# A causal mask as a minimum on VectorE, and another order of the small matmuls among the projection groups

## The chip, the cores and the metric

The kernel runs on one core of a Trainium2 chip. The metric is the time of one execution on the device, in microseconds (us). The engines are TensorE (PE in the rows; PEld is its weight load), VectorE (DVE), ScalarE (ACT), GpSimd (POOL) and SyncE (SP), which issues the DMAs here.

## What is computed

One decoder layer on 512 tokens of width 1024, float32. Cut to what matters:

```
h    = rms_norm(x, g_pre);  proj = h @ w_in        # 1664 RWKV columns, 1536 for q, k, v, 1024 gates
RWKV, 8 heads of 64, token by token:
   Sa = S a_t;  S = S * w_t + Sa b_t^T + v_t k_t^T;  y_t = S r_t
   then a norm per head, times lnx_w plus lnx_b, plus (r.k.r_k) v
attention, 8 heads of 64: logits = q k^T / 8 - slope * (t - s) for s <= t, else -1e30; softmax; times v
   (2 blocks of 256 with both always selected: plain causal attention)
y    = concat(y_rwkv, y_attn) * silu(gates)
out  = x + rms_norm(y @ w_out, g_post)
```

## The kernel before

Tokens lie along the free axis (512 columns) and features on the partitions, except for the attention's V and the output. A projection of 128 columns is made in full precision from two halves of each operand: weights and activations are split into a high part and a rest (`whi`, `wlo`, `xhi`, `xlo`), and three products are summed in PSUM (line 246). One product over 512 features, four matmuls of 128x512, is called a projection **group**; a projection of 128 columns is six groups. The split of a weight tile is a copy on ScalarE (line 230) and a subtraction on VectorE (line 231).

The RWKV half is done in chunks of 64 tokens. For each of four pairs of heads, `rwkv_keys` (line 359) makes decays and keys, with `ends` products for norms (396) and four transposes (405), and `rwkv_pairs` (423) makes the products within a chunk: transposes (437), products of 64x128 (444), the masked copy on VectorE (446), and two products for the bonus (462). `rwkv_inverse` (482) inverts 32x32 triangular blocks by a loop on VectorE, sends them through DRAM (502 to 511), and then **merges** the blocks by four quarters of 32x32 matmuls (514 to 534), each followed by copies on ScalarE and VectorE. `rwkv_chain` (542) takes eight steps, one per chunk: the state products (AR, 568), their copies, the u product (575) and its two copies (576, 577), the values of the next chunk (579), the update with BT (584), and the rest of the outputs (591).

The attention takes pairs of heads (`attn_pair`, 689): a stage for the row maxima (704 to 708), whose result is put into the operands, and then for each head and key block j the scores of 512-128j queries (732, 733), a mask product `tri` on the diagonal block (734), the exponential on ScalarE (736), and one step later the products with V (726). Afterwards four transposes and the gate (755).

The output projection (`half`, 820) runs in nine pieces of up to 512 columns, each with an RWKV half g=0 and an attention half g=1; `early_out` (833) issues the first half of pieces 0 and 1, the loop from line 892 the rest, with `AHEAD` pieces begun early.

TensorE's program order is written by a planner: the small parts are generators that yield (ns, wait), and `side` (107) resumes one when a virtual clock has reached its due time; `stream` (120) calls it after each projection group, at most two or three at a time. `PLAN` sets the order of the projections, and `PENDING` how many of them may be issued after q1 before the chain must be finished. The waits in the yields thus move instructions; TensorE then runs them in that order. The other engines' orders come from the framework's scheduler. PSUM slots are rings: two of p, three of s, two of c, one of r.

Of the kernel before, what the change touches and what calls it, by code (L numbers as in the profile page):

```python
# [9 lines left out]
F32 = mybir.dt.float32  # L10
# [27 lines left out]
PS = {"p": 2, "s": 3, "c": 2, "r": 1}  # L38
WARM = 9
PLAN = "k1 r1 k2 r2 k3 r3 v1 v2 v3 V q0 c0 G4 G5 q1 c1 q2 c2 G6 q3 c3 G7 G0 G1 G2 G3"  # L40
PENDING, AHEAD = 8, 5
MM = 232.0


# [1 line left out]
def hybrid_layer(ctx, tc, x, xt, params, ranks, w_in, w_v, w_out, g_post, out):  # L46
# [28 lines left out]
    def mps(tag="c"):  # L75
        return kept(pm, (512,), F32, tag, "ps_" + tag, PS[tag])
# [123 lines left out]

    dist = cst.tile([128, 10, 128], mybir.dt.bfloat16, name="dist")
    alibi = cst.tile([128, NH, NB], F32, name="alibi")
    tri = cst.tile([128, 2, 128], mybir.dt.bfloat16, name="tri")

    def attn_constants():
        for b in range(NB):
            o = b * (b + 1) // 2
            nc.gpsimd.iota(dist[:, o:o + b + 1, :], pattern=[[128, b + 1], [1, 128]], base=-256,
                           channel_multiplier=0, allow_small_or_imprecise_dtypes=True)
            nc.gpsimd.affine_select(out=dist[:, o + b, :], in_=dist[:, o + b, :], pattern=[[-1, 128]],  # L210
                                    compare_op=ALU.is_ge, fill=256.0 * NEG, base=0, channel_multiplier=1)
        nc.gpsimd.iota(alibi[:, 0, :], pattern=[[128, NB]], base=-256, channel_multiplier=1,
                       allow_small_or_imprecise_dtypes=True)
        for h in range(NH - 1, -1, -1):
            nc.vector.tensor_scalar(alibi[:, h, :], alibi[:, 0, :], 2.0 ** -(h + 1), None, ALU.mult)
        nc.vector.tensor_copy(tri[:, 0, :], ident)
        nc.gpsimd.memset(tri[:, 1, :], NEG)
        nc.gpsimd.affine_select(out=tri[:, 1, :], in_=tri[:, 1, :], pattern=[[-1, 128]], compare_op=ALU.is_gt,
                                fill=0.0, base=0, channel_multiplier=1)

    attn_constants()

# [136 lines left out]
    def rwkv_keys(p, ps):  # L359
# [2 lines left out]
        k = shifted(ps, 4 + p)  # L362
        sq = t2()
        nc.scalar.activation(sq, k, AF.Square, scale=col(KK + p))
        yield 0, 0 if p else 4000
        th = []
        for i in range(2):
            ps = mps()
# [19 lines left out]
        nc.scalar.activation(E[:, :, 1:C + 1], L.rearrange("p (c t) -> p c t", t=C), AF.Exp)  # L388
        en = at()
        nc.scalar.activation(en, L, AF.Exp, scale=-1.0)  # L390
        yield 4 * MM, 5500


        ps = mps()
# [28 lines left out]
    def rwkv_pairs(p, ps):  # L423
        g, q = p // 2, p % 2
        r = shifted(ps, p)
        yield 0, 0
        while keys[p] is None:
            yield 0, 300
        (k, E), BK = keys[p], BKs[:, q]
        ar, bt, am = AR[g][:, q], BT[g][:, q], Am[p]  # L430
        nc.vector.tensor_mul(ar[:, :, 1, :], v3(r), E[:, :, 1:C + 1])
        yield 0, max(4000, since[p] + 13000 - clock[0])
        msk = flat(mask).unsqueeze(1).to_broadcast([128, 4, 128])
        for c0 in (0, 4):
            ps = mps("r")
            for c in range(4):
                tr(ps[:, 128 * c:128 * c + 128], flat(BK[:, c0 + c]))
            acp(bt[:, c0:c0 + 4, :], ps.rearrange("p (c n) -> p c n", c=4))
            yield 900, 0
            pe = [mps("s") for _ in range(2)]  # L440
            for c in range(4):
                for e in range(2):
                    h = slice(64 * e, 64 * e + 64)
                    mm(pe[e][:, 128 * c:128 * c + 128], flat(BK[h, c0 + c]), flat(ar[h, c0 + c]), start=True, stop=True)
            for e in range(2):
                nc.vector.tensor_mul(am[:, e, c0:c0 + 4].rearrange("p c a b -> p c (a b)"),
                                     pe[e].rearrange("p (c n) -> p c n", c=4), msk)
            if c0:
                for hf in range(2):
                    d = slice(32 * hf, 32 * hf + 32)  # L450
                    nc.sync.dma_start(bd[hf, p].rearrange("n s t -> s n t"),
                                      am[d, :, :, 0, d].rearrange("s e c t -> s (e c) t"))
                paired[p] = True
            yield 1800, 2200
        nc.vector.scalar_tensor_tensor(r, r, col(RK + p), k, ALU.mult, ALU.mult)
        rk = [ring("kx", 2, T, dt=F32R) for _ in range(2)]
        acp(rk[0], r)
        nc.vector.tensor_sub(rk[1], r, rk[0].bitcast(F32))
        yield 0, 1500
        ps = mps("r")  # L460
        for i in range(2):
            mm(ps, bones_r, rk[i], start=(i == 0), stop=(i == 1))
        acp(bonus[p], ps)
        bon[p] = True
        yield 2 * MM, 0
# [16 lines left out]
    def rwkv_inverse():  # L482
# [31 lines left out]
        for g in range(2):  # L514
# [5 lines left out]
                           xq[0:32, 2 * g + q, e, c, :], start=True, stop=True)  # L520
            for e in range(2):
                (acp, vcp)[e](xq[32:64, 2 * g:2 * g + 2, e], px[64 * e + 32:64 * e + 64])
            yield 1700, 0
        for g in range(2):
            px = mps().rearrange("s (q c t) -> s q c t", q=2, t=32)
            for q in range(2):
# [4 lines left out]
            for q in range(2):  # L531
                for e in range(2):
                    (acp, vcp)[e](Am[2 * g + q][0:32, e, :, 0, 32:64], px[64 * e:64 * e + 32, q])
            yield 1700, 0
        ready["inverse"] = True
        yield 0, 800

# [4 lines left out]
    def rwkv_chain():  # L542
# [20 lines left out]
        for c in range(NCH):  # L563
# [5 lines left out]
                           stop=(s == 0 and p == NP - 1), skip_group_check=True)  # L569
            acp(uv[lo, 0], ry[0][lo])  # L570
            vcp(uv[lo, 1], ry[1][hi])
            yield 900 * (c > 0), 700
            u = mps()[:, 0:NP * HD].rearrange("p (q i) -> p q i", i=HD)
            for h, p, e in heads:
                mm(u[rows(e), p, :], Am[p][lo, e, c, 0, :], uv[lo, e, p, :], start=True, stop=True)
# [1 line left out]
            vcp(uv[lo, 1], u[hi])  # L577
            if not last:
                rn = values_in(c + 1)
            yield 500 + 1000 * (not last), 100  # L580
            if not last:
                d = mps()[:, 0:NP * HD].rearrange("p (q i) -> p q i", i=HD)
                for h, p, e in heads:
# [105 lines left out]
    def attn_pair(p):  # L689
# [29 lines left out]
        for e in range(2):  # L719
# [2 lines left out]
            PT = [None] * NB  # L722

            def times_values(j):
                for b in range(j, NB):
                    mm(po[:, b, 0:65], PT[j][:, 128 * (b - j):128 * (b - j) + 128], V[0][:, j, h, 0:65],
                       start=(j == 0 and b == 0), stop=(j == b), skip_group_check=True)

            for j in range(NB):
                n, cs = T - 128 * j, slice(128 * j, 128 * j + 128)  # L730
                ps = mps("s")
                mm(ps[:, 0:n], kx[e][:, cs], qx[e][:, 128 * j:T], start=True, stop=False)
                mm(ps[:, 0:n], kb[e][:, cs], qb[e][:, 128 * j:T], start=False, stop=False)
                mm(ps[:, 0:128], tri[:, 0, :], tri[:, 1, :], start=False, stop=True)
                PT[j] = t2()
                nc.scalar.activation(PT[j][:, 0:n], ps[:, 0:n], AF.Exp, scale=2.0 ** -(h + 1), bias=alibi[:, h, j:j + 1])  # L736
                yield 2 * MM * n / T + 80, 0
                if j:
                    times_values(j - 1)
                    yield 220 * (NB - j + 1), 0  # L740
# [67 lines left out]
    def out_weights():  # L808
        for k in range(8):
# [1 line left out]
                yield 0, 300  # L811
            wout(k)
            ready["wout"] = k
            yield 0, 1500

    xb = x[0].rearrange("(b p) d -> p b d", p=128)
    pieces = [(b, c) for b in range(NB) for c in ((0, 512), (512, 1024))][:-1] + [(NB - 1, (512, 768)), (NB - 1, (768, 1024))]
# [15 lines left out]
    def early_out():  # L833
# [4 lines left out]
            ys[0] = [t[:, i, :] for i in range(4)]  # L838
        for p in range(NP):
            gated(p, bonus[p])  # L840
        yield 0, 8000
        for i in range(2):
            for n in half(i, 0):
                yield 4 * MM, 0
# [51 lines left out]
    for b in range(NB):  # L896
# [2 lines left out]
        xs = [load_w(xb[:, b, 512 * n:512 * n + 512]) for n in range(2)]  # L899
        os = [at() for _ in range(2)]  # L900
        for j, i in enumerate(mine):
            if i + AHEAD < len(pieces):
                for n in half(i + AHEAD, 0):
                    pass
            for n in half(i, 1):
                pass
            cs = slice(*pieces[i][1])
            w, ps = cs.stop - cs.start, acc[i]
            sq = t2()
# [72 lines left out]
```

## Time and profile before

| | |
|---|---|
| median of three runs | 386.14 us (385.98 to 391.16) |
| profiled execution | 386.54 us, span 384.8 us |
| TensorE busy | 358.9 us (93% of the span) |
| VectorE, ScalarE, GpSimd busy | 243.7, 189.3, 32.8 us |
| chain that ended last | TensorE 80%, ScalarE 7%, VectorE 6% |
| mean granted clock of TensorE | 0.964 of 2.4 GHz |

The span runs from the first to the last instruction of the profiled execution. A time in square brackets behind an instruction is the idle time of its engine just before it, with what released it. Starts of matmuls are sharper than their durations, which overlap in the pipeline, so a rate is read from start to start.

### The profile page before, as it was taken

The numbers are of one execution on the slowest core, as the hardware profiler recorded it, in microseconds if no ns is written. First come the engines' busy times: TensorE is split into PE (matmuls) and PEld (weight loads), VectorE is DVE, ScalarE is ACT, GpSimd is POOL, SyncE is SP. The second block draws the span as 40 slices with busy tenths as digits, with TensorE's granted clock in tenths as the row PEclk, the third lists the DMA queues.
The fourth block names the chain that finished last, engine by engine and source line by source line (L and its number), as shares of the span: only waits on it lengthen the run. The fifth ranks groups of instructions, "written<-read, shape, count | busy, mean of one in ns | idle before, by whom it ended". The sixth has DMA issues, their size and how long they took to land.

```text
span 384.8 us, 7040 instructions
## 1 busy us (share of the span) xinstructions
PE 358.9 (93%) x2765; PEld 287.1 (75%) x2765; DVE 243.7 (63%) x521; ACT 189.3 (49%) x351; POOL 32.8 (9%) x55
## 2 busy tenths in 40 slices
PE   7999798999999999989999998889999989799893
PEld 3688576888877888877777775668888867688783
DVE  5976579859985999723544456884657961520344
ACT  5948855666654344632332357756457263510322
POOL 6000130012000000300000006222200000000000
PEclk9999998999999999976999996999999999989997
DMA  6830121321243223832111100110124401220334
GB/s 196 326 112 26 55 56 44 72 103 47 71 115 81 99 62 106 205 98 56 55 43 46 56 29 31 55 55 29 55 81 138 139 0 36 96 89 2 106 111 137
DMA packets 28321, 31.93 MB, mean 83 GB/s; under 512 B 12608, under 2 KB 15424, under 8 KB 28288
## 3 DMA queue, kind: packets, MB, share of 16 engines
q1 hardware_dynamic: 28288, 31.49, 27.0%
q8 instruction: 21, 0.34, 0.4%
q14 instruction: 12, 0.10, 0.1%
HBM read 28.07 MB, written 3.41 MB: 82 GB/s over the span
## 4 chain that ended last, share of the span: by engine, by line
PE 80%; ACT 7%; DVE 6%; issue 3%; DMA 1%; SPq 1%; POOL 1%; DVEq 0%; ACTq 0%
PE ps_p L92 38%; PE ps_s L92 23%; PE ps_c L92 12%; PE ps_r L92 4%; PE ps_r L95 3%; DMA AR_f<-in_xt_dram 1%; ACT t L736 1%; ACT BT_r L82 1%; DVE at L707 1%; PE ps_c L95 1%; DVE wlo L231 1%; POOL n L325 1%; ACT whi L82 1%; ACT BK_f L82 0%; SPq L153 0%
## 5 line engine op out<-in xcount | busy, mean ns | idle before, releaser
L92 PE MATMUL ps_p<-xhi_r,whi 128*128 128x512 f32 x200 | 58.3, 415 | 0.0
L92 PE MATMUL ps_p<-xlo_r,whi 128*128 128x512 f32 x200 | 57.9, 412 | 0.0
L92 PE MATMUL ps_p<-xhi_r,wlo 128*128 128x512 f32 x200 | 56.9, 407 | 0.0
L82 ACT ACTIVATE whi<-wraw 128x512 fp32r<-128x512 f32 x58 | 36.3, 628 | 39.1 <-PE ps_p L92 21.6
L231 DVE TENSOR_TENSOR wlo<-wraw,whi 128x512 fp32r<-128x512 f32 x58 | 39.9, 687 | 20.0 <-ACT whi L82 18.6
L92 PEld LDWEIGHTS ps_p<-xhi_r,whi 128*128 128x128 f32 x200 | 37.4, 196 | 7.8 <-issue 0.2
L92 PEld LDWEIGHTS ps_p<-xlo_r,whi 128*128 128x128 f32 x200 | 37.1, 195 | 7.6
L92 PEld LDWEIGHTS ps_p<-xhi_r,wlo 128*128 128x128 f32 x200 | 36.4, 191 | 7.4
L92 PE MATMUL ps_c<-V_f,t 128*128 128x65 f32 x160 | 22.7, 273 | 1.4 <-ACT t L736 1.4
L92 PEld LDWEIGHTS ps_c<-V_f,t 128*128 128x128 f32 x160 | 21.1, 192 | 3.1 <-ACT t L736 2.5
L736 ACT ACTIVATE t<-ps_s,alibi 128x512 f32<-128x512 f32 (+3 forms) x32 | 16.2, 523 | 10.6 <-PE ps_s L92 10.3
L92 PE MATMUL ps_s<-UV_f,Am_f 64*64 64x64 f32 x288 | 16.4, 238 | 0.0
L92 PEld LDWEIGHTS ps_s<-UV_f,Am_f 64*64 64x64 f32 x288 | 14.1, 150 | 1.2 <-issue 0.7
L82 ACT ACTIVATE Am_r<-wraw 128x512 fp32r<-128x512 f32 x16 | 9.9, 625 | 10.0 <-PE ps_s L92 6.0
L707 DVE CUSTOM_DVE_ANT_0 at<-ps_s,dist 128x128 f32<-128x128 f32 (+3 forms) x32 | 14.4, 486 | 0.4 <-PE ps_s L92 0.2
L803 DVE TENSOR_TENSOR UV_r<-wraw,Am_r 128x512 fp32r<-128x512 f32 x8 | 5.5, 685 | 14.2 <-ACT Am_r L82 14.2
L82 ACT ACTIVATE UV_f<-ps_c 64x512 f32<-64x512 f32 (+1 forms) x16 | 7.8, 485 | 13.6 <-PE ps_c L92 9.3
L325 POOL TENSOR_TENSOR n<-n,cols 128x8 f32<-128x8 f32 x4 | 7.8, 1943 | 75.5 <-DVE n L398 69.3
L92 PE MATMUL ps_s<-Am_r 128*128 128x128 f32 (+3 forms) x32 | 11.5, 367 | 1.4 <-ACT t L736 1.4
L92 PE MATMUL ps_p<-xhi_r,Am_r 128*128 128x512 f32 x32 | 10.9, 411 | 1.2 <-DVE Am_r L258 0.6
L82 ACT ACTIVATE t<-t,omm 128x512 f32<-128x512 f32 x13 | 9.3, 720 | 5.4 <-DVE t L319 4.6
L319 DVE TENSOR_TENSOR t<-ps_p,rinv 128x512 f32<-128x512 f32 x11 | 7.4, 681 | 5.7 <-PE ps_p L92 3.6
(305 smaller groups left out, 736.0 us busy)
## 6 DMA issues: line engine op xcount, KB each, us to landing
wraw<-in_w_in_dram SPq DMA_DIRECT2D x50, 256.0 KB, 2.9
wraw<-in_w_out_dram SPq DMA_DIRECT2D x16, 256.0 KB, 2.8
wraw<-in_w_v_dram SPq DMA_DIRECT2D x8, 256.0 KB, 3.0
wraw<-in_x_dram SPq DMA_DIRECT2D x8, 256.0 KB, 3.8
out_dram<-at SPq DMA_DIRECT2D x7, 256.0 KB, 2.0
AR_f<-in_xt_dram SPq DMA_DIRECT2D x4, 256.0 KB, 4.4
BT_f<-in_xt_dram SPq DMA_DIRECT2D x4, 256.0 KB, 6.3
BQ_f<-in_w_in_dram SPq DMA_DIRECT2D x4, 256.0 KB, 5.6
```

The source lines that it names most:

```text
L82: nc.scalar.activation(out, in_, AF.Copy, scale=scale)
L92: return tc.keep_in_program_order(nc.tensor.matmul(*args, **kw))
L95: return tc.keep_in_program_order(nc.tensor.transpose(out, in_, ident))
L231: eng.tensor_sub(lo, raw, hi.bitcast(F32))
L319: nc.vector.tensor_mul(q, ps, rinv)
L325: nc.gpsimd.tensor_tensor(y, x, cols[:, 3:4].to_broadcast(list(x.shape)), ALU.pow)
L707: nc.vector.tensor_tensor_reduce(at()[:, 0:n], ps[:, 0:n], dist[:, i:i + b + 1, :].rearrange("p j s -> p (j s)"), -1.0, 3.0e38, ALU.add, A ...
L736: nc.scalar.activation(PT[j][:, 0:n], ps[:, 0:n], AF.Exp, scale=2.0 ** -(h + 1), bias=alibi[:, h, j:j + 1])
L803: nc.vector.tensor_sub(lo, raw, hi.bitcast(F32))
```

## The change

The mask product is gone. In its place VectorE takes the minimum of the exponentials of the diagonal block with a constant that is 3e38 where s <= t and 0 elsewhere, in place; the products with V take the diagonal block last. The rest of the diff changes waits in the planner, the PSUM ring of one of two tiles in the second half of `rwkv_pairs`, `PENDING` from 8 to 9, the place of the early output halves, and the order of two halves in the output loop.

```diff
-PENDING, AHEAD = 8, 5
+PENDING, AHEAD = 9, 5
...
-    tri = cst.tile([128, 2, 128], mybir.dt.bfloat16, name="tri")
+    tri = cst.tile([128, 128], F32, name="tri")
...
-        nc.vector.tensor_copy(tri[:, 0, :], ident)
-        nc.gpsimd.memset(tri[:, 1, :], NEG)
-        nc.gpsimd.affine_select(out=tri[:, 1, :], in_=tri[:, 1, :], pattern=[[-1, 128]], compare_op=ALU.is_gt,
-                                fill=0.0, base=0, channel_multiplier=1)
+        nc.gpsimd.memset(tri, 3.0e38)
+        nc.gpsimd.affine_select(out=tri, in_=tri, pattern=[[1, 128]], compare_op=ALU.is_ge,
+                                fill=0.0, base=0, channel_multiplier=-1)
...
 # rwkv_keys
-        yield 0, 0 if p else 4000
+        yield 0, 0 if p else 5000
...
-        yield 4 * MM, 5500
+        yield 4 * MM, 6500
...
 # rwkv_pairs
-        yield 0, max(4000, since[p] + 13000 - clock[0])
+        yield 0, max(4000, since[p] + (13000 if p else 15000) - clock[0])
...
-            pe = [mps("s") for _ in range(2)]
+            pe = [mps("s"), mps("c" if c0 else "s")]
...
 # rwkv_inverse, at both loops over the merge's quarters
-            yield 1700, 0
+            yield 1700, 500
...
 # rwkv_chain
-            yield 900 * (c > 0), 700
+            yield 900 * (c > 0), 1000
...
-            yield 500 + 1000 * (not last), 100
+            yield 500 + 1000 * (not last), 0 if not last else 700
...
 # attn_pair
-                for b in range(j, NB):
+                for i, b in enumerate([*range(j + 1, NB), j]):
                     mm(po[:, b, 0:65], PT[j][:, 128 * (b - j):128 * (b - j) + 128], V[0][:, j, h, 0:65],
-                       start=(j == 0 and b == 0), stop=(j == b), skip_group_check=True)
+                       start=(i + j == 0), stop=(j == b), skip_group_check=True)
...
-                mm(ps[:, 0:n], kb[e][:, cs], qb[e][:, 128 * j:T], start=False, stop=False)
-                mm(ps[:, 0:128], tri[:, 0, :], tri[:, 1, :], start=False, stop=True)
+                mm(ps[:, 0:n], kb[e][:, cs], qb[e][:, 128 * j:T], start=False, stop=True)
                 PT[j] = t2()
                 nc.scalar.activation(PT[j][:, 0:n], ps[:, 0:n], AF.Exp, scale=2.0 ** -(h + 1), bias=alibi[:, h, j:j + 1])
-                yield 2 * MM * n / T + 80, 0
+                nc.vector.tensor_tensor(PT[j][:, 0:128], PT[j][:, 0:128], tri, ALU.min)
+                yield 2 * MM * n / T, 200
...
 # out_weights
-            yield 0, 1500
+            yield 0, 4000 if k < 4 else 1500
...
 # early_out
             gated(p, bonus[p])
-        yield 0, 8000
+            yield 0, 3000
+        yield 0, 3000
...
 # output loop
         for j, i in enumerate(mine):
+            for n in half(i, 1):
+                pass
             if i + AHEAD < len(pieces):
                 for n in half(i + AHEAD, 0):
                     pass
-            for n in half(i, 1):
-                pass
```

TensorE at the merge of the inverse (`ps_c` with `BK_f` and `Am_f`; groups have `ps_p`), one piece of the difference:

```order
-L92 MATMUL ps_c<-BK_f,Am_f 32x32 x64
+L92 MATMUL ps_c<-BK_f,Am_f 32x32 x32
+L92 MATMUL ps_p<-xhi_r,wlo 128x512 x4
+L92 MATMUL ps_c<-BK_f,Am_f 32x32 x32
+L92 MATMUL ps_p<-xlo_r,whi 128x512 x4
 L92 MATMUL ps_c<-Am_f,BK_f 32x32 x32
-L92 MATMUL ps_p<-xhi_r,wlo 128x512 x4
+L92 MATMUL ps_p<-xhi_r,whi 128x512 x4
 L92 MATMUL ps_c<-Am_f,BK_f 32x32 x32
+L92 MATMUL ps_p<-xhi_r,wlo 128x512 x4
 L92 MATMUL ps_s<-UV_f,Am_f 64x64 x16
```

A group stands behind each of the four quarters, where one stood behind the third.

TensorE in a chain step, from the state products' end over u (`ps_c<-UV_f,Am_f`) and the next values to the update with `BT_f`, one piece of the difference:

```order
+L92 MATMUL ps_p<-xhi_r,whi 128x512 x4
 L92 MATMUL ps_p<-xhi_r,wlo 128x512 x4
 L92 MATMUL ps_c<-UV_f,Am_f 64x64 x8
 L92 MATMUL ps_s<-UV_f,Am_f 64x64 x16
-L92 MATMUL ps_p<-xlo_r,whi 128x512 x4
 L92 MATMUL ps_c<-UV_f,BT_f 64x64 x8
```

The group between the values and the update now stands before u.

TensorE ahead of pairs(0), whose first transposes are `ps_r<-ident,BK_f`; `ps_c<-ident,t` are the transposes of keys(0) and keys(1), `ps_c<-qx,V_r` the rank products of keys(2). Before:

```order
103 L95 MATMUL ps_c<-ident,t 128x128 x4
104 L92 MATMUL ps_p<-xhi_r,wlo 128x512 x4
105 L95 MATMUL ps_c<-ident,t 128x128 x4
106 L92 MATMUL ps_p<-xlo_r,whi 128x512 x4
107 L92 MATMUL ps_p<-xhi_r,whi 128x512 x4
108 L92 MATMUL ps_p<-xhi_r,wlo 128x512 x4
109 L92 MATMUL ps_p<-xlo_r,whi 128x512 x4
110 L95 MATMUL ps_r<-ident,BK_f 128x128 x4
```

After the change:

```order
104 L95 MATMUL ps_c<-ident,t 128x128 x4
105 L92 MATMUL ps_p<-xlo_r,whi 128x512 x4
106 L95 MATMUL ps_c<-ident,t 128x128 x4
107 L92 MATMUL ps_p<-xhi_r,whi 128x512 x4
108 L92 MATMUL ps_p<-xhi_r,wlo 128x512 x4
109 L92 MATMUL ps_p<-xlo_r,whi 128x512 x4
110 L92 MATMUL ps_p<-xhi_r,whi 128x512 x4
111 L92 MATMUL ps_c<-qx,V_r 128x512 x4
112 L92 MATMUL ps_p<-xhi_r,wlo 128x512 x4
113 L95 MATMUL ps_r<-ident,BK_f 128x128 x4
```

One more group and the rank products with a group behind them have moved ahead of pairs(0).

## Rows read from the trace of the kernel before

**Rows 1.** windows of the span: bounds, length, busy us per engine (instructions), clock, DMA share, GB/s

```profile
75.00:117.00 42.00, 41.77 (x247) 33.89 (x245) 35.07 (x60) 26.43 (x49) 3.80 (x3) 1.00 0.31 86
243.00:259.00 16.00, 13.58 (x67) 9.91 (x67) 14.09 (x45) 9.47 (x18) 1.79 (x1) 1.00 0.15 46
308.00:337.00 29.00, 24.92 (x169) 20.71 (x168) 13.40 (x29) 15.59 (x31) 0.00 (x0) 0.99 0.14 46
```

**Rows 2.** windows, TensorE alone: bounds, length, busy us (instructions), granted clock, DMA share, GB/s

```profile
59.70:63.50 3.80, 3.80 (x22) 0.55 0.22 69
169.00:180.00 11.00, 9.93 (x154) 0.53 0.20 51
231.00:241.00 10.00, 8.39 (x49) 0.66 0.10 31
336.00:340.00 4.00, 3.90 (x12) 0.57 0.59 195
```

**Rows 3.** timeline of TensorE: start us, us, operation, count, idle before and its releaser

```profile
55.02 1.08 PE L92 MATMUL ps_p<-xhi_r,wlo 128*128 128x512 f32 x4
55.94 1.07 PE L92 MATMUL ps_p<-xlo_r,whi 128*128 128x512 f32 x4
59.13 0.66 PE L95 MATMUL ps_r<-ident,BK_f 128*128 128x128 f32 x4 [2.12 <-DVE BK_f L418]
```

**Rows 4.** timeline of VectorE at keys(1)

```profile
59.00 0.74 DVE L407 SCALAR_TENSOR_TENSOR yt<-t,prm,ps_c 128x512 f32<-128x512 f32 x1
59.65 0.68 DVE L231 TENSOR_TENSOR wlo<-wraw,whi 128x512 fp32r<-128x512 f32 x1
```

**Rows 5.** timeline of TensorE at the merge

```profile
164.10 2.21 PE L92 MATMUL ps_c<-BK_f,Am_f 32*32 32x32 f32 x128
166.71 1.20 PE L92 MATMUL ps_c<-Am_f,BK_f 32*32 32x32 f32 x64 [0.40 <-DVE BK_f L85]
170.11 1.92 PE L92 MATMUL ps_c<-Am_f,BK_f 32*32 32x32 f32 x64 [1.07 <-DVE Am_f L85]
```

**Rows 6.** line 510, copies back of the inverse: ns min/median/max, first and last start us

```profile
L510 SPq DMA_DIRECT2D Am_f<-qd x8: 337/487/1545, 157.5 to 162.8; - x8
```

**Rows 7.** timelines of TensorE, ScalarE and VectorE in one chain step

```profile
194.69 1.19 PE L92 MATMUL ps_p<-xhi_r,whi 128*128 128x512 f32 x4
195.81 0.69 PE L92 MATMUL ps_c<-UV_f,BT_f 128*64 128x64 f32 x16
...
193.43 0.63 ACT L82 ACTIVATE whi<-wraw 128x512 fp32r<-128x512 f32 x1 [0.73 <-PE ps_p L92]
194.11 0.38 ACT L82 ACTIVATE UV_f<-ps_c 64x256 f32<-64x256 f32 x1
...
194.09 0.69 DVE L231 TENSOR_TENSOR wlo<-wraw,whi 128x512 fp32r<-128x512 f32 x1 [1.30 <-ACT whi L82]
194.70 0.42 DVE L85 COPY UV_f<-ps_c 64x256 f32<-64x256 f32 x1
```

**Rows 8.** timeline of TensorE at the last u of the chain

```profile
233.24 0.68 PE L92 MATMUL ps_c<-UV_f,Am_f 64*64 64x64 f32 x16 [1.61 <-ACT UV_f L82]
```

**Rows 9.** timeline of TensorE at an attention head

```profile
260.09 0.23 PE L92 MATMUL ps_s<-tri 128*128 128x128 bf16 x1
260.13 0.42 PE L92 MATMUL ps_s<-qx,kx 128*128 128x384 f32 x1
```

**Rows 10.** line 707, row maxima: ns min/median/max, first and last start us, forms

```profile
L707 DVE CUSTOM_DVE_ANT_0 at<-ps_s,dist x32: 260/488/689, 242.8 to 313.6; 128x128 f32<-128x128 f32 x8, 128x256 f32<-128x256 f32 x8, 128x384 f32<-128x384 f32 x8, 128x512 f32<-128x512 f32 x8
```

**Rows 11.** timeline of TensorE at the end of the attention

```profile
331.24 1.11 PE L92 MATMUL ps_c<-V_f,t 128*128 128x65 f32 x8 [0.36 <-ACT t L736]
334.47 0.44 PE L92 MATMUL ps_c<-V_f,t 128*128 128x65 f32 x2 [0.34 <-ACT t L736]
336.11 1.00 PE L95 MATMUL ps_r<-ident,t 128*128 128x128 f32 x4 [1.20 <-DVE t L745]
```

**Rows 12.** timeline of TensorE in the output loop

```profile
363.20 0.74 PE L92 MATMUL ps_s<-Am_r,xhi_r 128*128 128x256 f32 x4 [1.56 <-DVE at L913]
```

More of the change, by code (lines that the diff above doesn't have):

```diff
@@ L533, in rwkv_inverse @@
                     (acp, vcp)[e](Am[2 * g + q][0:32, e, :, 0, 32:64], px[64 * e:64 * e + 32, q])
-            yield 1700, 0
+            yield 1700, 500
         ready["inverse"] = True
```

## The prediction

> **What bounds the kernel now.** I read first the page's shares (TensorE busy 93% of the span and 80% of the chain that ended last), then the table of stretches, then TensorE's timeline at each place where a stretch is not full. TensorE is the bound nearly everywhere: in 75 to 117 us it is busy 41.77 of 42 us [rows 1]. So time can be gained only by taking matmuls away, by closing its idle gaps, or by raising its clock. The gaps are few: 2.42 us of 16 in 243 to 259, 4.08 of 29 in 308 to 337 [rows 1], and single waits named below. The clock is the larger item: four stretches are granted a mean of 0.53 to 0.66 [rows 2]. As the clock has only its two levels, a stretch of width w and mean clock g holds w(1-g)/0.5 at 1.2 GHz, and half of that is lost: 1.7 us at 60 us, 5.2 at 169, 3.4 at 231, 1.7 at 336; 12.0 in all. Each of the four follows a wait: 2.12 us at 59.13 [rows 3], 0.40 and 1.07 us at the merge [rows 5], 1.61 us at 233.24 [rows 8], 1.20 us at 336.11 [rows 11]. A projection group costs 0.92 us start to start (55.02 to 55.94) [rows 3]; that is my unit for moved groups.
>
> **The change, part by part.**
>
> *Mask (-4.3).* 32 matmuls with the mask and their weight loads go. Each is shown busy 230 ns, but TensorE pipelines: the one at 260.09 is followed by the next matmul at 260.13 [rows 9]. The next also pays for the switch of weights; comparing such neighbours with and without a mask matmul I put one at 0.135 us (my estimate between the 0.04 of the start distance and the 0.23 of the busy time), so 32 x 0.135 = 4.3 us; the ends are 1.3 and 7.4. Half lie in 259 to 308, where TensorE is full, so they count whole. Added are 32 minimum operations of 128x128 on VectorE. Its nearest row is the row maximum, 260 ns at its shortest, the 128x128 form [rows 10]; with a hand-over some 0.4 us. Only the diagonal product waits for it, and it is now issued last; three, two and one products of about 0.28 us each (1.11 us for the four of the first block at 331.24 [rows 11]) stand ahead of it for the first three key blocks, none for the last, where up to 0.4 us per head can show. VectorE's own time, 32 x 0.3 = 10 us, costs nothing where it has room, and the max stage is where it has none (14.09 of 16 us in 243 to 259 [rows 1]).
>
> *Early part, pairs(0) (+2; ends -1 and +5).* The changed order has one more group before the `ends` products, and three groups' worth of work put ahead of pairs(0)'s transposes: two projection groups and keys(2)'s four products of the ranks. The second half of those four writes the PSUM slot that line 407 of keys(1) frees. That operation ran from 59.00 to 59.74 [rows 4], and the changed order puts two more splits of weights (0.68 us each [rows 4]) before it on VectorE, so I expect the slot at about 61.1 us. TensorE is there at about 56.9 (57.0 is where it began to wait before): 4.2 us of idle time in place of 2.12. Against that, pairs(0) then finds 3 x 0.92 = 2.76 us of work already done: 61.1 + 1.4 = 62.5, minus 2.76, against 59.13: 0.6 us behind. The half clock that follows the wait stays. A second place, the second product of pairs(0)'s `rk`, waits for line 457 on VectorE, which I place 2 us after TensorE gets there; in the kernel before nothing waited there. 0.6 + 2, less some slack, is +2. If VectorE keeps pace it is -1, if both waits come with another half-clock stretch it is +5.
>
> *Merge (-4.5; ends -6.6 and 0).* Now a group stands after each quarter of the merge. The copies after a quarter take 0.4 to 1.1 us to show [rows 5], one group is 0.92, so the two waits (1.47 us) go. If the clock then never falls, 5.2 us more come back. What is late next is the inverse's DMA: the eight copies of its result are issued until 162.8 [rows 6], 1.3 us before the merge starts at 164.10, and the change moves two groups from behind pairs(3) to ahead of it, so TensorE stands at the merge 1.8 us sooner relative to the inverse. Some 0.7 us of wait at the first quarter is my estimate, and the later quarters' data is covered by the groups between. I take the waits whole, the clock by some three fifths: -1.5 - 3.0.
>
> *Chain (+2; ends 0 and +9).* Two groups stand after the state products and two after the update, and none between u and BT. Before, u's two copies ended on ScalarE at 194.49 and on VectorE at 195.12, and BT started at 195.81 behind a group that began at 194.69 (1.12 us) [rows 7]. Without that group TensorE would be at BT at 194.69 and wait to 195.12: 0.43 us. Seven steps make 3.0; less about 0.15 per step for one switch fewer between large and small products, +2. What hides it entirely would be copies that are not behind a weight split; what makes it 9 is under the rivals.
>
> *End of the chain (-2; ends -5 and 0).* With nine groups pending one more stands before the last u: of the 1.61 us wait [rows 8] about 1.0 goes. Whether the half clock behind it (3.4 us) goes too is open; a third of it is taken.
>
> *Attention tail (+1; ends -2 and +4).* The 24 products of the output projection (24 x 0.23 = 5.5 us) that stand in the middle of the tail move behind the last transposes. The tail's other waits (0.34 at 334.47, 1.20 at 336.11 [rows 11]) then have no large matmuls between them, but the heads of the last two pairs now alternate. I give it +1 for the minimum on the last key block.
>
> *Output loop (-1.6).* The second half of a piece now precedes the first half of the piece five later, which was what waited 1.56 us for a PSUM slot at 363.20 [rows 12]. The work in between (2.8 us) covers it. The slower weight loads for the output (4000 for 1500) and the constants at the start cost nothing: the weights are loaded long before use.
>
> The sum: -4.3 + 2 - 4.5 + 2 - 2 + 1 - 1.6 = -7.4 us. The profiled execution took 386.54 us (span 384.8 and 1.7 around it), 0.4 above the median of 386.14; 386.5 - 7.4 = 379.1, so **379 us** against the median.
>
> At the clock I weigh a rule. The rows show a stretch with 2.42 us of idle time in 16 and a granted clock of 1.00 [rows 1], and half clock behind waits of over 1 us [rows 3, 5, 8, 11]. The Trainium skill, "TensorE: Matmul & The Clock Gate", section "A second HAM failure mode: psum-queue depth-cycling", says that an engine that idles briefly between groups often enough can swing between the two levels. By the rows the chain keeps 2.4 GHz through waits of 0.4 us; by the rule it would not, and the second rival below would be the likely case.
>
> **Rivals.** *(a) The early queue eats the gain.* VectorE is busy 35.07 of 42 us in 75 to 117 [rows 1], so what it loses at pairs(0) it does not soon make up; both early waits come (+5), the merge keeps its half clock (-1.5). -4.3 + 5 - 1.5 + 2 - 2 + 1 - 1.6 = -1.4: 385 us. For it: the hand-traced slot at 61.1. Against: the same wait before cost only one short stretch.
>
> *(b) Chain steps become the bound, slower than before.* If in each step the u copies stand behind a weight split on ScalarE (0.63 us at 193.43 [rows 7]) and on VectorE (0.69 at 194.09 [rows 7]), they end some 1.25 us after the values instead of 0.43: seven times that is 9 us. That alone gives 386.5 - 9.4 + 9 = 386, no change (9.4 is the gain of the other parts). It decides only if the clock falls too: the four groups of a step, 3.7 us, take as much again at 1.2 GHz, so from about two steps lost (386 + 7.4 = 393.5) it is slower, and with four it is 401 us. For it: the skill's rule above, and splits that stand right ahead of several u copies in the new order. Against: 1.00 through the waits of 243 to 259 [rows 1].
>
> *(c) Everything is hidden and the clock stays up.* Merge -6.6, end of chain -5, early 0, chain 0, tail 0: -4.3 - 6.6 - 5 - 1.6 = -17.5, 369 us. For it: each low stretch follows one wait that the change touches. Against: the early one gets longer. Halfway to it lies 374.
>
> *(d) The mask does not pay:* matmuls hidden in pipelining (1.3 instead of 4.3) and minimum operations that show, +3 and +2: 384 us.
>
> **How the numbers follow.** 2% either way, about what a measurement tells from no change, is below 378.4 and above 393.9. The forecast case (376 to 382) has 0.48, its middle close to the bound, so I count 0.23 of it as faster. Case (a) 0.15, (c) with its halfway form 0.23, (d) 0.08, (b) 0.06 of which 0.05 is over the bound. Faster 0.23 + 0.23 = 0.46, slower 0.05, same 0.49. The range of 371 to 387 leaves out the extreme of (c) and (b).
>
> **What would show it.** No mask matmuls, 32 minimum operations near 0.3 us, and 0.04 us less between products of one head. A wait at the four rank products near 57 us, released by line 406 of the changed kernel, of about 4 us. No wait over 0.5 us and a clock of 1.00 between the merge's quarters. In the chain, 0.4 us before BT, with VectorE's u copy as its releaser. No wait at the ninth half of the output loop. I am wrong if the chain shows a clock under 1.00, if the merge waits for DMA by more than 3 us, or if the tail without its filler idles more than 8 us.

## The result, and the profile after

The changed kernel takes 382.1 us (median of four runs, 381.44 to 382.56) beside 386.16 us of the kernel before on the same chip. The ratio is 0.9889 with a 95% interval of [0.9847, 0.9932]: faster by 1.1%, which the 2% bound calls no change. The forecast was 379, in a range of 371 to 387; the direction was right, the gain was 4.1 us instead of 7. The profiled execution took 381.44 us, the quickest of the four, with a span of 379.7 us, 5.1 less than before. Some executions, of the kernel before and of one run below, were slower throughout by some per cent; they are left out of the times and ratios that follow. On three other chips the kernel before has medians of 386.6 to 388.5 us, so kernels are compared below by their ratios to it.

Stretches of the changed kernel, columns as in [rows 1]:

```profile
180.00:230.00 50.00, 49.45 (x839) 38.83 (x835) 25.15 (x49) 17.43 (x38) 0.00 (x0) 1.00 0.15 48
230.00:243.00 13.00, 11.04 (x70) 8.29 (x66) 8.22 (x17) 11.63 (x22) 8.61 (x18) 0.87 0.13 43
259.00:308.00 49.00, 45.68 (x273) 38.65 (x271) 35.45 (x92) 25.91 (x47) 5.84 (x4) 1.00 0.25 81
```

VectorE has taken on 8.3 us of work (252.0 for 243.7 us in all). The chain's stretch is nearly full at 1.00, the end of the chain has 0.87 where it had 0.74 (by the same windows of before), and TensorE, which was full from 259 to 308 us before, now idles 3.32 us there. TensorE's windows at 1.2 GHz in which it had work:

```profile
61.30:64.70 3.40, 3.35 (x10) 0.50 0.05 19
235.40:238.80 3.40, 3.40 (x20) 0.50 0.47 159
327.50:330.90 3.40, 3.40 (x11) 0.51 0.69 221
```

Three stretches of 3.4 us stand where there were four of 3.4, 9.2, 6.8 and 3.4 busy us [rows 2]. The one at the merge is gone and the one behind the chain is halved. At most half of the busy time at 1.2 GHz is lost: 5.1 us for 11.4. Idle time (span less TensorE's busy time) went the other way: 28.0 us for 25.9. So busy time fell by 7.2 us (351.7 for 358.9), of which at most 6.3 us is clock, and the rest the mask products. **The gain is clock and missing mask products; the change made TensorE wait more, not less.**

TensorE's timeline: the two early places, the merge, one chain step, the last u.

```profile
61.35 1.19 PE L92 MATMUL ps_c<-qx,V_r 128*128 128x512 f32 x2 [3.65 <-DVE yt L406]
78.58 0.51 PE L92 MATMUL ps_r<-kx,bones_r 128*128 128x512 f32 x1 [0.90 <-DVE kx L457]
...
165.97 1.20 PE L92 MATMUL ps_c<-BK_f,Am_f 32*32 32x32 f32 x64
167.10 1.20 PE L92 MATMUL ps_p<-xhi_r,wlo 128*128 128x512 f32 x4
168.22 1.20 PE L92 MATMUL ps_c<-BK_f,Am_f 32*32 32x32 f32 x64
170.47 1.20 PE L92 MATMUL ps_c<-Am_f,BK_f 32*32 32x32 f32 x64
172.73 1.20 PE L92 MATMUL ps_c<-Am_f,BK_f 32*32 32x32 f32 x64
...
195.31 0.68 PE L92 MATMUL ps_c<-UV_f,BT_f 128*64 128x64 f32 x14 [0.27 <-DVE UV_f L85]
232.25 0.68 PE L92 MATMUL ps_c<-UV_f,Am_f 64*64 64x64 f32 x16 [0.17 <-ACT UV_f L82]
```

These answer to [rows 3], [rows 5], [rows 7] and [rows 8]. The early wait has grown from 2.12 to 3.65 us and has the releaser that the prediction named (line 406); the second one, 0.90 us, is there too. Not forecast was that the wait before the `ends` products would fall from 1.44 to 0.41 us. The merge's quarters follow at 2.25 us, each with a group between, and wait for nothing. A group among them takes 1.12 us from start to start (167.10 to 168.22), more than the 0.92 that the prediction put on a moved group. In the chain 0.27 us before BT is left, in two of seven steps only. The last u waits 0.17 us.

In the attention and at its end (the first two rows are in the stretch that was full before):

```profile
272.75 0.85 PE L92 MATMUL ps_c<-V_f,t 128*128 128x65 f32 x6 [0.35 <-DVE t L744]
274.96 0.44 PE L92 MATMUL ps_c<-V_f,t 128*128 128x65 f32 x2 [1.36 <-DVE t L735]
...
325.48 0.66 PE L92 MATMUL ps_c<-V_f,t 128*128 128x65 f32 x4 [1.02 <-DVE t L735]
327.43 1.00 PE L95 MATMUL ps_r<-ident,t 128*128 128x128 f32 x4 [1.29 <-DVE t L744]
```

The minimum operations themselves are what was expected, 291 ns each, and line 735's two rows say who waited for them:

```profile
L735 DVE TENSOR_TENSOR t<-t,tri x32: 281/291/294, 260.7 to 325.3; 128x128 f32<-128x128 f32 x32
  PE ps_c L92: 2.7, 3
```

VectorE ahead of those two waits:

```profile
274.01 0.69 DVE L615 TENSOR_TENSOR BK_f<-BK_f,gn 128x512 f32<-128x512 f32 x1 [1.41 <-POOL gn L324]
274.62 0.48 DVE L735 TENSOR_TENSOR t<-t,tri 128x128 f32<-128x128 f32 x2
...
324.54 0.69 DVE L784 TENSOR_TENSOR xlo_r<-at,xhi_r 128x512 fp32r<-128x512 f32 x1
325.14 0.49 DVE L735 TENSOR_TENSOR t<-t,tri 128x128 f32<-128x128 f32 x2
```

At 274.01 line 615 (the norm of the RWKV output) starts after VectorE has stood 1.41 us, waiting for the power operation on GpSimd. The minimum that TensorE needs is the first of the two behind it in VectorE's order; it ends at 274.9, and TensorE starts at 274.96. At 325.14 the minimum comes behind a 0.69 us operation of the gate. A mask product stood in no such queue. The row maxima wait longer too, 3.4 us in all for 1.5; the run without the minimum (below) has 3.8 us of these waits, so they come from the order and not from the minimum.

The output loop has no wait at the ninth half. From the last transposes to the end of the span it took 48.0 us before (336.76 to 384.8), and 51.6 now (328.08 to 379.7) with 24 more products in it (5.5 us): 46.1, a gain of 1.9.

### The profile page after: what moved, and what is told of

It reads as the page before. It is cut to its first block, busy times and chain, and to the rows that moved or that the text cites. A ratio compares the mean times of both kernels' runs of the same rounds, so it can differ in the third digit from the quotient of the medians.

```text
span 379.7 us, 7003 instructions
## 1 busy us (share of the span) xinstructions
PE 351.7 (93%) x2733; PEld 283.7 (75%) x2733; DVE 252.0 (66%) x552; ACT 188.5 (50%) x351; POOL 32.1 (8%) x55
## 4 chain that ended last, share of the span: by engine, by line
PE 53%; DVE 6%; ACT 5%; issue 3%; POOL 1%; POOLq 0%; DVEq 0%; ACTq 0%
PE ps_p L92 24%; PE ps_s L92 15%; PE ps_c L92 8%; PE ps_r L92 4%; PE ps_r L95 2%; DVE at L706 1%; ACT BT_r L82 1%; POOL gn L324 1%; ACT t L734 1%; ACT whi L82 1%; DVE UV_r L802 1%; DVE t L735 1%; ACT AR_r L82 1%; POOLq L977 0%; DVE wlo L230 0%
## 5 line engine op out<-in xcount | busy, mean ns | idle before, releaser
L92 PE MATMUL ps_p<-xhi_r,whi 128*128 128x512 f32 x200 | 56.2, 404 | 0.0
L92 PE MATMUL ps_p<-xlo_r,whi 128*128 128x512 f32 x200 | 55.8, 401 | 0.0
L92 PEld LDWEIGHTS ps_p<-xhi_r,wlo 128*128 128x128 f32 x200 | 37.4, 193 | 7.9
L92 PEld LDWEIGHTS ps_p<-xlo_r,whi 128*128 128x128 f32 x200 | 36.0, 188 | 7.4
L92 PE MATMUL ps_c<-V_f,t 128*128 128x65 f32 x160 | 21.9, 270 | 3.2 <-DVE t L735 2.7
L92 PE MATMUL ps_s<-UV_f,Am_f 64*64 64x64 f32 x288 | 15.0, 224 | 0.3 <-ACT UV_f L82 0.3
L92 PEld LDWEIGHTS ps_s<-UV_f,Am_f 64*64 64x64 f32 x288 | 12.6, 135 | 1.5 <-ACT UV_f L82 0.7
L735 DVE TENSOR_TENSOR t<-t,tri 128x128 f32<-128x128 f32 x32 | 9.0, 289 | 4.6 <-ACT t L734 3.9
L913 DVE TENSOR_TENSOR at<-ps_p,yt 128x512 f32<-128x512 f32 x2 | 1.4, 686 | 15.7 <-ACT t L910 15.7
L320 DVE SCALAR_TENSOR_TENSOR t<-t,prm 128x511 f32<-128x511 f32 x13 | 9.7, 750 | 2.8 <-ACT t L82 2.7
```

Of the source, the lines that this page charges most:

```text
L92: return tc.keep_in_program_order(nc.tensor.matmul(*args, **kw))
L320: nc.vector.scalar_tensor_tensor(t[:, 1:T], q[:, 0:T - 1], col(MU + m), t[:, 1:T], ALU.mult, ALU.add)
L735: nc.vector.tensor_tensor(PT[j][:, 0:128], PT[j][:, 0:128], tri, ALU.min)
L913: nc.vector.tensor_mul(os[cs.start // 512][:, cs.start % 512:cs.start % 512 + w], ps, gpb[:, cs])
```

## The experiments

All times are medians; ratios are to the kernel before on the same chip. Where the intervals of two ratios overlap, the times do not tell the two kernels apart, and what is said of their difference rests on the traces.

**The mask products out, nothing in.** Edit: line 734 deleted; the constants and the order of the products with V (diagonal block last) are those of the change, everything else is as before.

> The kernel before in its own order of instructions, with the 32 mask products taken out and nothing put in their place (so the attention is left unmasked). It gives the price of the mask on TensorE alone. Theory P (the prediction's term: 0.135 us each): 386.1 - 4.3 = 381.8 us. Theory R (TensorE pays only the 0.04 us from start to start): 386.1 - 1.3 = 384.8 us. Theory W (TensorE waits elsewhere in the attention, so the freed time turns into waits): over 385.5 us, with larger waits on the exponentials and the row maxima.

Measured: 384.0 us, ratio 0.9926 [0.9886, 0.9966], that is -2.9 us with ends of -1.3 and -4.4: 0.09 us per product (0.04 to 0.14). The prediction's 0.135 is at the edge, and the waits on the exponentials grew (0.49, 0.54 and 0.48 us where they were 0.30 to 0.36), which is theory W in part.

**The minimum in the old order.** Edit: as the run above, with the minimum put in; the piece that replaces the mask product:

```diff
-                mm(ps[:, 0:128], tri[:, 0, :], tri[:, 1, :], start=False, stop=True)
+                nc.vector.tensor_tensor(PT[j][:, 0:128], PT[j][:, 0:128], tri, ALU.min)
                 yield 2 * MM * n / T + 80, 0
```

> The same order as in the run without a mask, with the minimum on VectorE put in and the diagonal product last. Theory P: about 0.4 us per head at most, some 1 us more than the run without a mask, 382.8. Theory Q (the minimum stands in VectorE's queue behind operations that wait for GpSimd or ScalarE): 2 to 4 us more than the run without a mask, with waits of over 1 us on line 735 before a diagonal product.

Measured: 396.7 us, ratio 1.0278 [1.0223, 1.0332], 12.7 us more than without a mask: far beyond both theories in size, and Q in kind. TensorE, then VectorE ahead of each of its two largest waits:

```profile
272.15 0.69 PE L92 MATMUL ps_c<-V_f,t 128*128 128x65 f32 x2 [2.40 <-DVE t L735]
316.49 0.69 PE L92 MATMUL ps_c<-V_f,t 128*128 128x65 f32 x2 [2.78 <-DVE t L735]
...
270.27 0.69 DVE L615 TENSOR_TENSOR BK_f<-BK_f,gn 128x512 f32<-128x512 f32 x1 [1.66 <-POOL gn L324]
270.88 0.42 DVE L744 TENSOR_TENSOR t<-ps_c,rs 128x256 f32<-128x256 f32 x1
271.21 0.68 DVE L230 TENSOR_TENSOR wlo<-wraw,whi 128x512 fp32r<-128x512 f32 x1
271.81 0.28 DVE L735 TENSOR_TENSOR t<-t,tri 128x128 f32<-128x128 f32 x1
...
314.32 1.29 DVE L784 TENSOR_TENSOR xlo_r<-at,xhi_r 128x512 fp32r<-128x512 f32 x2
315.53 0.68 DVE L706 CUSTOM_DVE_ANT_0 at<-ps_s,dist 128x512 f32<-128x512 f32 x1
316.14 0.49 DVE L735 TENSOR_TENSOR t<-t,tri 128x128 f32<-128x128 f32 x2
```

The first is again line 615 behind GpSimd; the second minimum stands behind two splits of the gate and a row maximum. TensorE idles 32.7 us for 26.5. With these waits its clock is low for 38.5 busy us for 20.2, and the same matmuls keep it busy for 362.9 us instead of 355.4, another 7.5 us. So in the old order the mask edit makes the kernel slower by 2.8%.

**The changed kernel without its minimum.** Edit: the minimum deleted from the changed kernel.

> The changed kernel without its 32 minimum operations (the attention is left unmasked). Theory P: the minimum is nearly hidden, 382.1 - 1 = 381.1 us. Theory Q: the waits on line 735 (2.7 us in the profile of the changed kernel) and their followers go, 382.1 - 3 = 379 us, and the half clock behind the last transposes may go with them.

Measured: 380.3 us, ratio 0.9827 [0.9775, 0.9878], beside 0.9889: by the ratios the minimum costs 2.4 us in the new order. Q is nearer than P, but the intervals overlap, so the size is not sure.

**The early edits taken back in the changed kernel** (4000, 5500, 13000, both tiles from ring s).

> The changed kernel with the four edits to rwkv_keys and rwkv_pairs taken back (4000, 5500, 13000, both tiles from ring s). The prediction's term for them was a loss of 2 us and the two traces show TensorE 1.9 us later at the first merge products: so 382.1 - 1.9 = 380.2 us. Rival: the later start of the merge was what let the copies of the inverse land, so a wait for DMA of 1 to 2 us comes in its place and the time stays at 382.

Measured: 383.2 us, ratio 0.9899 [0.9847, 0.9951]: no difference. The mechanism holds: idle time fell from 28.0 to 26.1 us. But its profile has four half-clock stretches with 13.7 us of work for 10.2, which is 1.7 us back. The rival named, a wait for DMA at the merge, did not come.

**The order alone** (mask products back, the rest of the change kept).

> The changed kernel with the mask products back on TensorE (mask, order of the products with V and the yields of the attention as before), all other edits kept. Theory P (prediction: the mask change gains 3 us): 382.1 + 3 = 385 us. Theory Q (the products cost 2 us and the minimum's waits cost 2.5): the same as the changed kernel or a little faster, 381.5 us, with no idle time on line 735 and TensorE idle for 2 to 3 us less than the 28.0 us of the changed kernel.

Measured: 382.9 us, ratio 0.9897 [0.983, 0.9963], the same as with the mask edit (0.9889). So on this order the mask edit is not shown to be worth anything: the ratios differ by 0.3 us, and the 3 us of theory P lie near the edge of what the two intervals allow. Idle time was 27.8 us and not 2 to 3 less, so Q was wrong there: the waits on line 735 are replaced by others, seven of 0.30 to 0.99 us on the exponential.

**Order alone without the early edits.**

> As the run with the mask products back, and the four edits to rwkv_keys and rwkv_pairs taken back too: merge, chain, nine pending, late early halves and the order of the output loop are left of the change. If each part that lost time is gone, TensorE idles about 24 us (28.0 - 2.5 - 1.9), and the time is 380 us, the fastest so far. Rival: idle time is not what sets the time, the half-clock stretches are, and they come back in another place: 382 to 384 us.

Measured: 378.9 us, ratio 0.9784 [0.9737, 0.983]: the fastest of all, and clear of the changed kernel's interval. Idle time was 24.5 us, as expected. One half-clock stretch is left up to 374 us:

```profile
46.90:53.70 6.80, 6.80 (x21) 0.50 0.11 39
53.70:374.00 320.30, 305.49 (x2570) 1.00 0.25 76
```

It is also 4.0 us faster than the run with the mask products back, measured on the same chip, and each of its six executions is faster than each of the other's. Not all of the 4 us is due to the early edits. Here the planner also puts the 24 early output products ahead of the last transposes, not behind them, so the wait of 1.2 us that the run with the mask products back had there is covered (see the run with the tail put back, below).

**The merge's waits back to 0 in the changed kernel.**

> The changed kernel with the waits of 500 behind the merge's quarters back to 0, so that quarters follow each other. The prediction's term (-4.5, at most -6.6): 382.1 + 4.5 = 386.6 us, with waits of 0.4 and 1.1 us on the copies and a half-clock stretch of some 9 us behind them. Rival: the wait alone comes back (1.5 us) and the clock stays up, 383.6 us.

Measured: 384.4 us, ratio 0.9931 [0.9897, 0.9965], 1.6 us slower than the changed kernel by the ratios, with intervals that overlap. At the merge it has the first of the two waits again (the second did not come), and the half-clock stretch, with 10.2 us of work:

```profile
169.78 1.92 PE L92 MATMUL ps_c<-Am_f,BK_f 32*32 32x32 f32 x64 [0.40 <-DVE BK_f L85]
...
174.02 1.92 PE L92 MATMUL ps_c<-Am_f,BK_f 32*32 32x32 f32 x64
```

From the last group ahead of the merge to the chain's first u it took 14.7 us for 13.1 with three groups fewer in it, a loss of 4.3 to 4.9 us (a group counted at 0.91 to 1.12). But the groups that the merge no longer used filled waits later, and idle time fell to 25.7 us. Both theories had the place right and the end result wrong.

**No power operation on GpSimd.** Edit: the call of `rsqrt` in `rwkv_norm` deleted, the sum of squares used in its place.

> The changed kernel without the four power operations of GpSimd in the norm of the RWKV output (line 324; the norm's scale is then wrong), so that VectorE's line 615 waits for nothing on GpSimd; the order of all other instructions is the same. Theory Q: the minimum at 275 us is no longer behind that wait, the 1.36 us of TensorE at the diagonal product and the 0.35 us before it go, 382.1 - 1.7 = 380.4 us. Theory S (the minimum is late because of its own exponential): the wait of 1.36 us stays and the time is 382.

Measured: 380.4 us, ratio 0.9846 [0.9772, 0.9921], and the waits of 0.35 and 1.36 us are gone. VectorE and TensorE at the same place:

```profile
271.01 0.68 DVE L614 TENSOR_TENSOR BK_f<-BK_f,gn 128x512 f32<-128x512 f32 x1
271.61 0.49 DVE L734 TENSOR_TENSOR t<-t,tri 128x128 f32<-128x128 f32 x2
...
271.74 1.00 PE L92 MATMUL ps_c<-V_f,t 128*128 128x65 f32 x8
274.23 0.78 PE L92 MATMUL ps_c<-V_f,t 128*128 128x65 f32 x6
```

Line 614 here is line 615 there: without GpSimd it starts at 271.01, the two minimum operations follow at 271.61, and the products with V run without idle time. Theory Q is shown for this wait; S falls. In time alone the run is not told apart from the changed kernel.

**Merge and output loop alone, in the kernel before.**

> The kernel before with two of the change's edits alone: the waits of 500 behind the merge's quarters, and the second half of a piece ahead of the first half of a later one in the output loop. By the decomposition of the two traces these carry nearly all of the gain: 1.5 us of waits and up to 4.6 us of half clock at the merge, 1.56 us in the output loop. So 386.2 - 1.5 - 3 - 1.6 = 380 us, a ratio of 0.984. If the other edits carried the gain instead (mask, chain, nine pending), 384 us.

Measured: 389.9 us, ratio 1.0055 [1.0011, 1.0099]: slower than before, the clearest miss. At the merge itself it gained as much as the changed kernel, some 5 us: TensorE's rows there are the same. Behind it the time went to waits and to the clock; the two largest waits:

```profile
234.66 0.81 PE L92 MATMUL ps_c<-UV_f,Am_f 64*64 64x64 f32 x16 [2.91 <-ACT UV_f L82]
313.49 0.74 PE L92 MATMUL ps_s<-Am_r 128*128 128x512 f32 x1 [3.78 <-DVE mx L707]
...
308.89 1.29 DVE L783 SCALAR_TENSOR_TENSOR at<-bonus,AR_f 128x512 f32<-128x512 f32 x2
310.10 0.68 DVE L783 SCALAR_TENSOR_TENSOR at<-bonus,E 128x512 f32<-128x512 f32 x1
310.73 1.90 DVE L785 TENSOR_TENSOR xlo_r<-at,xhi_r 128x512 fp32r<-128x512 f32 x3
312.54 0.68 DVE L783 SCALAR_TENSOR_TENSOR at<-bonus,E 128x512 f32<-128x512 f32 x1
```

The three groups that went into the merge are missing later, so instructions behind it have other neighbours. The last u waits 2.91 us for ScalarE (it was 1.61), and a product of the row maxima waits 3.78 us for VectorE, which is busy from 308.89 with the gating of `early_out`: seven of its 0.69 us operations in a row (neighbours of one line share a row), all issued at once. The change spreads them by `yield 0, 3000` between the pairs, and no run that has this edit shows such a wait; the edit was not tried alone, and the prediction gave it no term. Smaller waits are new or longer there (1.05 and 1.19 us on the row maxima, 1.00 on an exponential). Work at 1.2 GHz is 23.1 us, as before (22.8): the stretch at the merge is gone, those at 47 and 341 us are longer and one at 313.6 us is new. The one at 47 us, ahead of all that was edited, accounts for the 2.1 us by which this profile is behind before the merge.

**Two of the early edits in again, on the fastest.**

> As the fastest run so far (mask products back, the early edits back), but with two of the four early edits in again: 5000 and 6500 in rwkv_keys. They put one group ahead of the ends products; the edit that put the rank products of keys(2) ahead of pairs(0) stays out. Expected: the idle time before the ends products falls by 0.9 us, and no wait of 3.6 us comes: 378.9 - 0.9 = 378.0 us; 376 if the half clock at 47 us goes too. Rival: the group moved ahead is missing at pairs(0), and the wait there grows by the same 0.9: 378.9.

Measured: 379.6 us, ratio 0.9799 [0.9752, 0.9847]: no difference. The wait before the `ends` products fell from 1.44 to 0.41 us, and the two at pairs(0) (1.01 and 1.47 us) became one of 3.33, 0.85 us more, as the rival said:

```profile
60.21 1.12 PE L95 MATMUL ps_r<-ident,BK_f 128*128 128x128 f32 x4 [3.33 <-DVE BK_f L418]
```

**The early output halves back in the middle of the tail, on the fastest.**

> As the fastest run so far, but with the early output halves due as before the change, so that their 24 products stand in the middle of the attention's tail instead of between its last products and its last transposes. Expected: the wait of 1.2 us at the last transposes comes back, and perhaps the half clock behind it (1.7 us): 378.9 + 1.2 to 2.9 = 380 to 382 us. If the place of these products does not matter, 379.

Measured: 380.9 us, ratio 0.9827 [0.9768, 0.9886], 1.7 us slower by the ratios, with intervals that overlap. The wait at the last transposes is back, without a half-clock stretch:

```profile
333.42 0.66 PE L95 MATMUL ps_r<-ident,t 128*128 128x128 f32 x4 [1.20 <-DVE t L745]
```

**The chain's waits back, on the fastest.**

> As the fastest run so far, but with the chain's waits as before (700 and 100), so that a group stands between the values and the update. The prediction's term was a loss of 2 us for taking it away, the trace of the changed kernel shows two waits of 0.27 us in seven steps: so 378.9 - 0.5 = 378.4, no difference that can be measured. By the prediction's term it would be 377. The waits of 0.27 us are to go.

Measured: 381.6 us, ratio 0.9838 [0.977, 0.9907]; 2.1 us slower by the ratios (the intervals overlap), where 0.5 faster was expected. The waits of 0.27 us went. But the last u waits 2.91 us and 6.8 us at half clock follow. TensorE, and ScalarE ahead of it:

```profile
234.35 0.68 PE L92 MATMUL ps_c<-UV_f,Am_f 64*64 64x64 f32 x16 [2.91 <-ACT UV_f L82]
...
232.12 1.26 ACT L82 ACTIVATE AR_r<-t 64x512 fp32r<-64x512 f32 x2
233.40 0.63 ACT L82 ACTIVATE whi<-wraw 128x512 fp32r<-128x512 f32 x1
233.93 0.36 ACT L82 ACTIVATE UV_f<-ps_s 64x256 f32<-64x256 f32 x1
```

In the fastest kernel the same u waits 0.18 us:

```profile
231.92 0.68 PE L92 MATMUL ps_c<-UV_f,Am_f 64*64 64x64 f32 x16 [0.18 <-ACT UV_f L82]
...
231.50 0.36 ACT L82 ACTIVATE UV_f<-ps_s 64x256 f32<-64x256 f32 x1
231.76 1.26 ACT L82 ACTIVATE AR_r<-t 64x512 fp32r<-64x512 f32 x2
```

With two groups behind the last state products, ScalarE's order has the copy for u ahead of two splits of an attention operand (1.26 us) and a weight split (0.63); with one group it has it behind them. So the edit to the chain is what closes the wait at its end, and nine pending alone does not.

## Why the prediction came out as it did

The parts, measured between equal points of TensorE's program in the two profiles (a projection group that is the same in both; the matmuls that stand on the other side of the point are counted at their usual rate, which leaves a part open by some half a microsecond):

| part | forecast | measured |
|---|---|---|
| early part, up to the group before the merge (162.19 to 164.06) | +2 | +1.9 |
| merge | -4.5 | -5.2 |
| chain | +2 | +0.6 |
| end of chain, up to the last row maxima of the first pairs | -2 | -1.6 |
| mask and attention tail (the rest) | -4.3 + 1 | +1.1 |
| output loop | -1.6 | -1.9 |
| sum | -7.4 | -5.1 |

The sum is that of the two profiled executions, the quickest of four for the changed kernel; by the medians it is -4.1.

**The step that failed is the mask.** It was priced as matmuls that go, and as minimum operations that cost "nothing where it has room". The matmuls were worth 2.9 us instead of 4.3: 0.09 us each, between the two ends given. The minimum cost 2.4 us by the ratios of two runs whose intervals overlap, and 12.7 us, clear of all noise, in the old order. That is not its 0.29 us or the 0.4 per head: it costs by what stands ahead of it, which the run without the power operation shows for the largest of these waits, 1.36 us. So the term of -4.3 + 1 came out near nothing. VectorE's busy share said nothing of that; its order did, and so did the trace of the kernel before, where the same operation (line 616 there) stands with VectorE idle 1.53, 1.75 and 1.75 us ahead of it, waiting for GpSimd, in the middle of the attention (timeline of VectorE):

```profile
267.05 0.69 DVE L616 TENSOR_TENSOR BK_f<-BK_f,gn 128x512 f32<-128x512 f32 x1 [1.53 <-POOL gn L325]
270.30 0.69 DVE L616 TENSOR_TENSOR BK_f<-BK_f,gn 128x512 f32<-128x512 f32 x1 [1.75 <-POOL gn L325]
274.69 0.69 DVE L616 TENSOR_TENSOR BK_f<-BK_f,gn 128x512 f32<-128x512 f32 x1 [1.75 <-POOL gn L325]
```

The prediction looked at VectorE's queue at pairs(0) and not here. The rival "the mask does not pay" had the cause in general words and 384 us; by sum it was nearer than the forecast, 1.9 us off instead of 3.1. Its parts were partly right: the products were not as cheap as its 1.3 us, and the minimum did show.

**The early part was right in place and releaser**, 3.65 us forecast as 4.2; the second wait was 0.90 us instead of 2, so that the sum of +1.9 for +2 is in part luck. **The merge was right**, waits and clock, and no DMA wait came, not even the 0.7 us allowed for. Its clock came back whole, where the prediction counted three fifths of 5.2 us. The term still came near because the 5.2 was too much: the prediction took half of the time at 1.2 GHz as lost, but a quarter of the merge takes 1.92 us there [rows 5] and 1.20 at 2.4 GHz, so less than half is lost on it. **The chain's loss was overestimated**: 0.27 us in two steps instead of 0.43 in seven, so the group that stood between u and the update had hidden little. The 0.15 us per step for a switch had no row behind it, and no run measures it. **The end of the chain was right in size, wrong in cause**: the term credited the ninth pending group; the last u waits 2.91 us with nine pending and the chain's old waits, 0.18 with nine and the new ones (0.66 at most in the runs beside it). What nine pending does by itself was not tried.

**The sum itself hides a rule that the prediction used in one place only**: groups are conserved. It counted the early groups as work already done, but at the merge, the end of the chain and the tail it took each wait closed as a gain. The run with the merge and the output loop alone shows how far that can fail: some 5 us gained at the merge and the result slower than before.

**Of the rivals**, slow chain steps (b) fall: the granted clock is 1.00 from 180 to 230 us with 0.55 us of idle time there. So the swing between levels that the Trainium skill's page "TensorE: Matmul & The Clock Gate" (section "A second HAM failure mode: psum-queue depth-cycling") describes for brief idles between groups is not seen in the chain at 0.27 us per wait. Behind the chain, three waits of 0.17, 0.27 and 0.47 us between 232 and 235 us are all that precedes the 1.2 GHz stretch at 235.4; but the fastest run has the same three (0.18, 0.28 and 0.47) and a granted clock of 1.00 there. The prediction took waits of over 1 us for the condition. It had looked only at those that a drop followed: in the kernel before the clock also stayed at 1.00 behind 1.44 us at 309.90, and in the changed kernel behind 1.36 us at 274.96. What decides is open. Rival (a), 385 us, had VectorE's early queue right, but the merge kept its gain.

## What to carry to other kernels

Work that moves from the full engine to one with room must be priced by what stands ahead of it in that engine's order, above all an operation that itself waits for a third engine; the busy share does not tell. Where fill work is put between dependent steps, ask from where it is taken and what will stand bare there, and cost the edits that mend that place as part of the same change. Before keeping a bundle of edits, take them out one by one, and then together those that gave nothing: here neither the mask nor the early order, taken out alone, changed the time, and without both the kernel is at 378.9 us, a ratio of 0.9784, in part because the early output products moved with them.

## What the runs showed of the hardware

The place of a half-clock stretch is not fixed by the instruction order. Up to pairs(0) the kernel before and all seven runs without the early edits have the same TensorE order and the same wait of 1.44 us before the `ends` products; the first fell to 1.2 GHz at 59.8 us for 3.4 us, the others at 46.7 to 49.1, for 3.4 to 6.8 us. The runs come from several chips, but executions of one kernel on one chip differ too: the changed kernel took 381.44 us at a mean clock of 0.985 and 382.0 to 382.6 at 0.976; the run without a mask, 381.5 to 386.6 at 0.973 to 0.960. The price of such a stretch is less than half of its work: the run without a mask and that with the minimum in the old order have the same 2733 matmuls, and 18.3 us more of work at 1.2 GHz made TensorE's busy time 7.5 us longer, 0.41 us for each. A single profile therefore tells a kernel's time to about 1% here, and idle time and clock are better read apart.
